# First conditioning in five steps of 2, 4, 4, 4 and 2 k-tiles, with the small loads on another queue and another transpose of x

## The chip, the cores and the metric

The kernel runs on one core of a Trainium2 chip. Its engines are TensorE (PE in the views; PEld is its weight load), VectorE (DVE), ScalarE (ACT), GpSimd (POOL) and SyncE (SP, which here only issues transfers). The metric is the device time of one launch in microseconds (us), the median of several runs.

## The reference, cut to what matters

One decoder block on 256 rows (SEQ) of width 2048 (D_MODEL), everything in float32. The change touches only the beginning: the conditioning vector c gives shifts, scales and gates through one large matrix, and the first of two SwiGLU networks reads the normalised and modulated x.

```python
def rms_norm(x, g):
    xf = x.astype(jnp.float32)
    y = xf * lax.rsqrt(jnp.mean(xf * xf, -1, keepdims=True) + EPS)
    return (y * g.astype(jnp.float32)).astype(x.dtype)
def modulate(x, g, shift, scale):
    return rms_norm(x, g) * (1 + scale) + shift
def swiglu(x, w_gate, w_up, w_down):
    return (jax.nn.silu(x @ w_gate) * (x @ w_up)) @ w_down
...
cond = jax.nn.silu(c)
ada = (cond @ w_ada[l] + b_ada[l]).reshape(B, N_ADA, 1, D)
sh1, sc1, gt1, sh2, sc2, gt2, sh3, sc3, gt3 = [ada[:, i] for i in range(N_ADA)]
h = modulate(x, g_norm[l, 0], sh1, sc1)
x = x + 0.5 * gt1 * swiglu(h, w_ffn_gate[l, 0], w_ffn_up[l, 0], w_ffn_down[l, 0])
```

The contraction of both w_ffn_gate and w_ffn_up runs over the 2048 columns of h, that is over 16 k-tiles of 128. A k-tile of h needs its own 128 shifts and 128 scales, which need all 2048 rows of 256 columns of w_ada.

## The kernel before

**Units.** Weights come in pieces of two k-tiles by 512 columns (512 KB), each into one of six `raw` buffers (`RAW`). ScalarE rounds a piece to its high part `whi` (L135), VectorE forms the low part `wlo` (L136), and TensorE multiplies: for each of two row halves of x and each of two k-tiles, the products whi·ahi, wlo·ahi and whi·alo (L215 to L217 from the function `unit`, L620 to L622 in `early`). That is 12 matmuls of 128x512, called a unit below. Four pairs of `whi` and `wlo` exist (`PREP`).

**Conditioning.** A piece of w_ada is not multiplied on TensorE: VectorE multiplies it by one column of cond and adds it to an accumulator `aacc` (L342 for the first of 16 row tiles, L344 for the other 15). At the end TensorE sums `aacc` over the partitions by matmuls with a column of ones (L379), VectorE adds the bias and the gain (L372, L373, result `mod`), and the function `mk` makes ahi (ScalarE, L717), the same in full (L719) and alo (VectorE, L724) from the transposed x. Such a chain of 16 pieces, a reduction and a `mk` is one step of the conditioning.

**Steps.** `STEPS` cuts the 16 k-tiles of the first network into four steps of four. Before the first step nothing can be multiplied. While the matmuls of one step run (nine half-chunks of weights, `EARLY`, so 18 units for four k-tiles), the 16 w_ada pieces of the next step are dealt out between the units by `interleave`, whose last two arguments (`LEAD`) say how many pieces are given at the outset. The first two half-chunks stay in PSUM over all steps, the other seven are emptied after each step (L625 on ScalarE after the first step, L627 on VectorE, which adds them up, after later ones).

**Order.** The program order is written out by hand: every engine works through its instructions in the order in which `run` emits them. `run` prepares pieces up to four ahead of the unit that is emitted (`AHEAD`), and a "bar" item holds preparation back at one place. A transfer into a `raw` buffer is issued by SP when the piece six before it has been used up.

**The beginning.** SP issues the loads of the identity, c, x and the w_ada pieces, and between these the eight small loads (biases, gains and positions, `load_small`, L299). ScalarE squares x (L434); the reduction, GpSimd's power and two diagonal matrices `dg` follow (`rstd_first`, L692 on VectorE), and `turn` multiplies x by `dg` on TensorE, which scales and transposes in one (L705). `small_cols` transposes the small loads (L304) and copies them (L305, L306).

Of the kernel before, what the change touches and what calls it, by code (L numbers as in the profile page):

```python
# [18 lines left out]
P = 128  # L19
D = 2048  # L20
# [15 lines left out]

LEAD = (0,3)
BAR, BARS = (2,0)
FILL = (4, 40, 320, 50, 60, 10)
XN = (0,14,0)  # L40
MK = 1
POOLN = 0
# [5 lines left out]
GAPS = (2, 4, 3, 2)  # L48
STEPS = ((0,4),(4,4),(8,4),(12,4))
C_ID, C_D, C_BC, C_MC, C_END = 0, 128, 384, 384 + 2 * HEADS * NCMP, 384 + 2 * HEADS * NCMP + 2 * NCMP  # L50
# [22 lines left out]
def block_kernel(ctx: ExitStack, tc: tile.TileContext, I, konst, decay, out):  # L73
# [10 lines left out]
    def act_hi(dt=F32R):  # L84
        return ap_.tile([P, 4, S], dt, tag="ahi", name="ahi")
# [30 lines left out]

    items, micro, held = [], deque(), []

# [15 lines left out]
    def split(raw_ap, hi_ap, lo_ap):  # L134
        nc.scalar.activation(hi_ap, raw_ap, AF.Copy)  # L135
        nc.vector.tensor_tensor(lo_ap, raw_ap, hi_ap.bitcast(F32), op=ALU.subtract)  # L136

    def run():
# [26 lines left out]
        def prep():  # L165
            i = st["prep"]
            kind, _, nk, n, fn = stream[i]
            raw = raws.pop(i)
            if kind == "w":
                hi = wp.tile([P, 2 * NCH], F32R, tag="whi", name="whi")  # L170
                lo = wp.tile([P, 2 * NCH], F32R, tag="wlo", name="wlo")
                split(raw[:, :nk * n], hi[:, :nk * n], lo[:, :nk * n])
                parts[i] = shaped(hi, nk, n), shaped(lo, nk, n)
                st["w"] += 1
            else:
                fn(raw[:, :nk * n])
            freed.add(i)
            st["prep"] += 1
            dma()
# [101 lines left out]
    nc.tensor.transpose(ps0[:, 0:16], r0[0:16], ident[0:16, 0:16])  # L281
    nc.scalar.activation(cond, ps0[:, 0:16], AF.Silu)

    def load_more():
# [13 lines left out]
                   (r2[102:118], I["ret_gn_gain"][0].rearrange("h (a p) -> (h a) p", p=P))]  # L298
    load_small = [("do", lambda to=to, frm=frm: nc.sync.dma_start(to, frm)) for to, frm in load_small]  # L299

# [19 lines left out]
    def rsqrt_mean(o, ssq, n):  # L320
# [3 lines left out]
        nc.gpsimd.tensor_tensor(o, o, mhalf[:, :w], op=ALU.pow)  # L324

    for t in range(2):
        nc.sync.dma_start(x[:, t], x_d[t * P:(t + 1) * P, :])
# [235 lines left out]
    def ffn(l, his, los, last, first=None, head=None):  # L563
# [84 lines left out]
        if first:  # L648
            its += first(*STEPS[0])
            for i, (k0, nk) in enumerate(STEPS):  # L650
                w = [it for ci in range(EARLY) for it in early(ci, k0, nk)]
                if i + 1 < len(STEPS):
                    w = interleave(w, first(*STEPS[i + 1]), int(len(w) * SPREAD), *LEAD)
                its += w
# [27 lines left out]

    big = cp.tile([P, 2, D], F32, tag="big", name="dg")
    dg = big[:, 0, :S].rearrange("p (t s) -> p t s", t=2)

    def rstd_first():
        for t in range(2):
            for n in range(4):
                square(t, n)
        r = rstd_x()  # L690
        for t in range(2):
            nc.vector.tensor_scalar(dg[:, t], ident, r[:, t:t + 1], None, op0=ALU.mult)  # L692

    h1, l1 = [], []

    def first(k0, nk):
        banks = []

        def turn():

            for k in range(nk):
                if k % 2 == 0:
                    banks.append(mx([P, 2, S]))
                for t in range(2):
                    nc.tensor.matmul(banks[-1][:, k % 2, t * P:(t + 1) * P], x[:, t, (k0 + k) * P:(k0 + k + 1) * P],  # L705
                                     dg[:, t], start=True, stop=True)

        def mk():
            h32 = t4([P, 4, S])
            for k in range(nk):  # L710
                kt = k0 + k
                if kt % 4 == 0:
                    h1.append(act_hi())
                    l1.append(act_lo())
                a, b = mod[:, 1, kt:kt + 1], mod[:, 0, kt:kt + 1]
                xT = banks[k // 2][:, k % 2]
                nc.scalar.activation(h1[-1][:, kt % 4], xT, AF.Identity, scale=a, bias=b)  # L717
                if MK:
                    nc.scalar.activation(h32[:, k], xT, AF.Identity, scale=a, bias=b)  # L719
                else:  # L720
                    nc.vector.tensor_scalar(h32[:, k], xT, a, b, op0=ALU.mult, op1=ALU.add)
                if k % 2:
                    ks = slice(kt % 4 - 1, kt % 4 + 1)
                    nc.vector.tensor_tensor(l1[-1][:, ks], h32[:, k - 1:k + 1], h1[-1][:, ks].bitcast(F32), op=ALU.subtract)  # L724
        o = ada_cols(0, k0, nk, True)
        if k0 == 0:
            o.insert(XN[1], ("do", small_cols))
            o.insert(XN[0], ("do", rstd_first))
            o = [i for it in zip(load_small, o) for i in it] + o[len(load_small):]
        if k0 == STEPS[1][0]:  # L730
            o.insert(5, ("do", load_more))
        o.insert(len(o) - 1 - XN[2], ("do", turn))
        return o + [("do", mk)] + ([("bar", BAR)] if k0 < BARS else [])

# [514 lines left out]
```

## Time and profile before

| | us |
|---|---|
| median of three runs | 2503.04 (2503.02 to 2503.77) |
| profiled execution, its own time | 2505.49 |
| its span, first to last instruction | 2503.7 |
| TensorE busy in the span | 2445.5 (98%) |
| VectorE busy | 1737.4 (69%) |
| ScalarE busy | 1140.9 (46%) |
| mean granted TensorE clock | 0.996 |

How to read it: the span is shorter than the execution by 1.8 us at its ends. TensorE is busy nearly throughout, so what shortens the kernel is its idle time, and its matmuls at the lower clock. A timeline row gives the start, the time from start to end of the merged instructions, the engine, the line, the operation and how many were merged; in brackets stand the idle time of the engine ahead of it and what ended that. Matmuls overlap in the rows: the time of one in a stream is the difference of the starts, 0.216 us at the higher level of the clock.

### The profile page before, as it was taken

To read this page: it belongs to the slowest core of one execution; us is meant where nothing else is said; L and a number is where in the kernel's file an instruction comes from. 1 tells how busy PE (TensorE), PEld (TensorE's weight loads), DVE (VectorE), ACT (ScalarE), POOL (GpSimd) and SP (SyncE) were. 2 spreads that over 40 slices of the span, in tenths; PEclk is the share of its full clock that TensorE was granted. 3 is DMA by queue.
4 is the path that set the end of the run, shared out by engine and by line. 5 is a ranking of instruction groups with operands and counts; after the bars stand their busy time and mean duration, and the time that the engine had idled before them with its cause. 6 is when DMAs were issued, how large, how long until landed. Compare 5 with 4: busy or idle time off the path is not lost. (4 is left out here: it accounts for less than half of the span.)

```text
span 2503.7 us, 31546 instructions
## 1 busy us (share of the span) xinstructions
PE 2445.5 (98%) x11616; PEld 2120.0 (85%) x11616; DVE 1737.4 (69%) x1968; ACT 1140.9 (46%) x1416; POOL 233.5 (9%) x201
## 2 busy tenths in 40 slices
PE   4999999999999999999999999999999999999999
PEld 4888888888887888888888888888788888888888
DVE  7898777898756466776767777776688555555555
ACT  3545444444445355554444444444544444444443
POOL 0000000110002133320000000001100010001001
PEclk9999999999999999999999999999999999999999
DMA  9998888899866455667888877887499666666664
GB/s 347 350 321 277 280 301 293 305 311 344 280 222 196 140 158 143 185 195 261 280 264 262 256 246 235 294 273 250 153 320 352 198 203 199 200 199 203 200 202 153
DMA packets 348339, 616.64 MB, mean 246 GB/s; under 512 B 22044, under 2 KB 80018, under 8 KB 347928
## 3 DMA queue, kind: packets, MB, share of 16 engines
q1 hardware_dynamic: 348184, 614.63, 74.8%
q8 instruction: 91, 1.49, 0.2%
q14 instruction: 64, 0.52, 0.1%
HBM read 612.45 MB, written 2.10 MB: 245 GB/s over the span
## 5 line engine op out<-in xcount | busy, mean ns | idle before, releaser
L136 DVE TENSOR_TENSOR wlo<-raw,whi 128x1024 fp32r<-128x1024 f32 (+1 forms) x865 | 1082.1, 1260 | 575.4 <-ACT whi L135 570.4
L135 ACT ACTIVATE whi<-raw 128x1024 fp32r<-128x1024 f32 (+1 forms) x865 | 906.9, 1056 | 1002.2 <-PE accb L217 730.6
L215 PE MATMUL accb<-whi,ahi 128*128 128x512 f32 x3232 | 1240.5, 384 | 6.1 <-ACT ahi L494 4.7
L216 PE MATMUL accb<-wlo,ahi 128*128 128x512 f32 x3232 | 1229.4, 380 | 3.8 <-DVE wlo L136 3.5
L217 PE MATMUL accb<-whi,alo 128*128 128x512 f32 x3232 | 1228.4, 380 | 2.9 <-DVE alo L541 1.5
L215 PEld LDWEIGHTS accb<-whi,ahi 128*128 128x128 f32 x3232 | 612.8, 190 | 95.1 <-ACT ahi L494 5.5
L216 PEld LDWEIGHTS accb<-wlo,ahi 128*128 128x128 f32 x3232 | 613.0, 190 | 92.2 <-DVE wlo L136 8.0
L217 PEld LDWEIGHTS accb<-whi,alo 128*128 128x128 f32 x3232 | 612.7, 190 | 92.5 <-DVE alo L541 1.9
L344 DVE SCALAR_TENSOR_TENSOR aacc<-raw,cond,aacc 128x1024 f32<-128x1024 f32 x270 | 354.2, 1312 | 1.3 <-DMA raw<-in_w_ada_dram 0.6
L558 POOL TENSOR_TENSOR x<-x,t 128x512 f32<-128x512 f32 x50 | 80.9, 1639 | 1156.2 <-DVE t L556 989.0
L621 PE MATMUL accb<-wlo,ahi 128*128 128x512 f32 x224 | 87.1, 389 | 2.5 <-DVE wlo L136 2.5
L620 PE MATMUL accb<-whi,ahi 128*128 128x512 f32 x224 | 86.7, 387 | 0.0
L622 PE MATMUL accb<-whi,alo 128*128 128x512 f32 x224 | 85.9, 384 | 0.0
L621 PEld LDWEIGHTS accb<-wlo,ahi 128*128 128x128 f32 x224 | 43.0, 192 | 12.1 <-DVE wlo L136 6.2
L540 ACT ACTIVATE ahi<-mx 128x512 fp32r<-128x512 f32 x52 | 28.1, 593 | 53.9 <-PE mx L449 53.9
L541 DVE TENSOR_TENSOR alo<-mx,ahi 128x512 fp32r<-128x512 f32 x52 | 33.4, 684 | 27.2 <-ACT ahi L540 27.2
L620 PEld LDWEIGHTS accb<-whi,ahi 128*128 128x128 f32 x224 | 43.1, 192 | 6.1
L622 PEld LDWEIGHTS accb<-whi,alo 128*128 128x128 f32 x224 | 43.0, 192 | 6.0
L556 DVE TENSOR_TENSOR t<-accb,gt 128x512 f32<-128x512 f32 x56 | 36.3, 683 | 7.7 <-PE accb L217 7.6
L787 ACT ACTIVATE t<-accb 128x512 f32<-128x512 f32 x52 | 30.1, 593 | 24.2 <-PE accb L217 24.1
L1004 ACT ACTIVATE t<-t,m 128x256 f32<-128x256 f32 (+1 forms) x64 | 28.3, 443 | 26.0 <-DVE m L994 26.0
L1113 POOL TENSOR_SCALAR rs<-bmv 128x2 f32<-128x2 f32 x8 | 1.8, 220 | 395.3 <-DVE bmv L1112 395.2
(182 smaller groups left out, 1025.6 us busy)
## 6 DMA issues: line engine op xcount, KB each, us to landing
raw<-in_w_ada_dram SPq DMA_DIRECT2D x288, 512.0 KB, 5.5
raw<-in_w_ffn_gate_dram SPq DMA_DIRECT2D x176, 512.0 KB, 5.1
raw<-in_w_ffn_up_dram SPq DMA_DIRECT2D x176, 512.0 KB, 4.7
raw<-in_w_ffn_down_dram SPq DMA_DIRECT2D x176, 512.0 KB, 4.2
raw<-in_w_in_dram SPq DMA_DIRECT2D x176, 512.0 KB, 4.5
raw<-in_w_in_dram SPq DMA_DIRECT2D x128, 256.0 KB, 3.9
raw<-in_w_proj_nsa_dram SPq DMA_DIRECT2D x32, 512.0 KB, 5.7
raw<-in_w_proj_ret_dram SPq DMA_DIRECT2D x32, 512.0 KB, 5.4
```

The costliest lines, as they stand in the source:

```text
L135: nc.scalar.activation(hi_ap, raw_ap, AF.Copy)
L136: nc.vector.tensor_tensor(lo_ap, raw_ap, hi_ap.bitcast(F32), op=ALU.subtract)
L215: nc.tensor.matmul(ps[t], xh, wh, start=kt == 0, stop=False)
L216: nc.tensor.matmul(ps[t], xh, wl, start=False, stop=False)
L217: nc.tensor.matmul(ps[t], xl, wh, start=False, stop=kt == K - 1)
L344: nc.vector.scalar_tensor_tensor(box[0], raw, k, box[0], op0=ALU.mult, op1=ALU.add)
L541: nc.vector.tensor_tensor(lo[:, 2 * b:2 * b + 2], ps, h.bitcast(F32), op=ALU.subtract)
L556: nc.vector.tensor_tensor(in_two(y), halves(ps[t]), in_two(gt[:, n * NCH:(n + 1) * NCH]), op=ALU.mult)
L558: (nc.vector if last and n == 3 else nc.gpsimd).tensor_tensor(xs, xs, y, op=ALU.add)
L620: nc.tensor.matmul(ps, xh, h, start=i == 0, stop=False)
L621: nc.tensor.matmul(ps, xh, l, start=False, stop=False)
L622: nc.tensor.matmul(ps, xl, h, start=False, stop=i == nk - 1)
```

## The change

Five things are changed together, all at the beginning of the program.

- `STEPS` becomes (0,2), (2,4), (6,4), (10,4), (14,2): five steps. In the first and last step the w_ada pieces are 2 x 256 columns (256 KB, runs of 1 KB instead of 2 KB) and each half-chunk has one unit. `LEAD` is given for each step; the second step's pieces get no head start.
- The eight small loads are issued by ScalarE's queue, ahead of the Silu that makes cond. `small_cols` and the squares become the first items of the program.
- x is scaled by ScalarE (`xs`, with the column rx) and transposed plainly against the identity, in place of the product with a diagonal matrix. The reduction of the squares stands behind six w_ada pieces on VectorE.
- Twelve matmuls of ones by ones, whose result nobody reads, stand behind the first transposes (`WARM`).
- In the first step `mk` forms alo for one k-tile at a time, and the first weight piece's wlo is emitted inside it; the bar now holds one piece behind the first step only.

```diff
-LEAD = (0,3)
-BAR, BARS = (2,0)
+LEAD = ((0, 0), (0, 3), (0, 3), (0, 3))
+BAR = 1
+WARM = 12
-XN = (0,14,0)
-MK = 1
+XN = (2, 5)
-STEPS = ((0,4),(4,4),(8,4),(12,4))
+STEPS = ((0, 2), (2, 4), (6, 4), (10, 4), (14, 2))
...
-                split(raw[:, :nk * n], hi[:, :nk * n], lo[:, :nk * n])
+                if st["w"]:
+                    split(raw[:, :nk * n], hi[:, :nk * n], lo[:, :nk * n])
+                else:
+                    nc.scalar.activation(hi[:, :nk * n], raw[:, :nk * n], AF.Copy)
+                    first_lo.append(lambda: nc.vector.tensor_tensor(
+                        lo[:, :nk * n], raw[:, :nk * n], hi[:, :nk * n].bitcast(F32), op=ALU.subtract))
...
-    load_small = [("do", lambda to=to, frm=frm: nc.sync.dma_start(to, frm)) for to, frm in load_small]
+    for to, frm in load_small:
+        nc.scalar.dma_start(to, frm)
...
+    nc.scalar.activation(cond, ps0[:, 0:16], AF.Silu)
...
+    def rms_first():
+        nc.vector.tensor_reduce(rx, ss, axis=AX.X, op=ALU.add)
+        rsqrt_mean(rx, rx, D)
...
+            ks = slice(k0 * P, (k0 + nk) * P)
+            for t in range(2):
+                nc.scalar.activation(xs[:, t, ks], x[:, t, ks], AF.Copy, scale=rx[:, t:t + 1])
             for k in range(nk):
                 if k % 2 == 0:
                     banks.append(mx([P, 2, S]))
                 for t in range(2):
-                    nc.tensor.matmul(banks[-1][:, k % 2, t * P:(t + 1) * P], x[:, t, (k0 + k) * P:(k0 + k + 1) * P],
-                                     dg[:, t], start=True, stop=True)
+                    nc.tensor.transpose(banks[-1][:, k % 2, t * P:(t + 1) * P],
+                                        xs[:, t, (k0 + k) * P:(k0 + k + 1) * P], ident)
+            if k0 == 0:
+                ps = mx()
+                for _ in range(WARM):
+                    nc.tensor.matmul(ps, ones_r, ones_r[:, None, :].to_broadcast([P, 4, P]), start=True, stop=True)
...
+            n = 1 if k0 == 0 else 2
...
+                while first_lo:
+                    first_lo.pop()()
...
+        if k0 == 0:
+            o.insert(XN[1], ("do", turn))
+            o.insert(XN[0], ("do", rms_first))
+            o = [("do", small_cols), ("do", lambda: [square(t, n) for t in range(2) for n in range(4)])] + o
+            return o + [("do", mk), ("bar", BAR)]
+        o.insert(len(o) - 1, ("do", turn))
+        return o + [("do", mk)]
```

Where the instructions stand: first VectorE from the program's beginning to the first low part of weights (`rx` is the column of 1/rms, `dg` the diagonal matrices, `cols` the small loads). Before:

```order
L438 TENSOR_REDUCE rx<-ss 128x2
L692 TENSOR_SCALAR dg<-kc,rx 128x128 x2
L342 TENSOR_SCALAR aacc<-raw,cond 128x1024
L344 SCALAR_TENSOR_TENSOR aacc<-raw,cond,aacc 128x1024 x15
L136 TENSOR_TENSOR wlo<-raw,whi 128x1024
```

The multiplications of the w_ada pieces stood behind the norm of x. And after, the same place on VectorE:

```order
L310 COPY cols<-mx 128x128 x2
L311 TENSOR_SCALAR gq<-cols 128x1
L348 TENSOR_SCALAR aacc<-raw,cond 128x512
L350 SCALAR_TENSOR_TENSOR aacc<-raw,cond,aacc 128x512 x5
L693 TENSOR_REDUCE rx<-ss 128x2
L350 SCALAR_TENSOR_TENSOR aacc<-raw,cond,aacc 128x512 x10
L378 TENSOR_TENSOR mod<-mx,cols 128x2x2
L379 SCALAR_TENSOR_TENSOR mod<-mod,cols 128x2
L176 TENSOR_TENSOR wlo<-raw,whi 128x1024
```

They now stand behind the small loads, each has half the columns, and the norm has moved behind the sixth. Second, SP's queue from the load of x on. Before, once the first step's pieces and the small loads are issued:

```order
L162 DMA raw<-in_w_ffn_gate_dram 128x2x512
L162 DMA raw<-in_w_ada_dram 128x2x512 x4
L162 DMA raw<-in_w_ffn_gate_dram 128x2x512
L162 DMA raw<-in_w_ada_dram 128x2x512
L162 DMA raw<-in_w_ffn_up_dram 128x2x512
```

One w_ada piece of the next step came with each unit's weights. After:

```order
L333 DMA x<-in_x_dram 128x2048 x2
L162 DMA raw<-in_w_ada_dram 128x2x256 x16
L162 DMA raw<-in_w_ffn_gate_dram 128x2x512
L162 DMA raw<-in_w_ada_dram 128x2x512 x2
L162 DMA raw<-in_w_ffn_up_dram 128x2x512
L162 DMA raw<-in_w_ada_dram 128x2x512 x2
```

In the first step now two w_ada pieces come with each unit's weights: 16 pieces of the next step with nine units instead of with 18.

## Rows read from the trace of the kernel before

**Rows 1.** The page, busy time of the engines over the span.

```profile
PE 2445.5 (98%) x11616; PEld 2120.0 (85%) x11616; DVE 1737.4 (69%) x1968; ACT 1140.9 (46%) x1416; POOL 233.5 (9%) x201
```

**Rows 2.** Timeline, the beginning: start, length, engine, line, operation, count.

```profile
6.52 0.63 ACT L434 ACTIVATE t<-x 128x512 f32<-128x512 f32 x1 [2.71 <-DMA x<-in_x_dram]
...
12.85 0.48 DVE L692 TENSOR_SCALAR dg<-kc,rx 128x128 f32<-128x128 f32 x2 [1.11 <-POOL rx L324]
...
14.03 19.77 DVE L344 SCALAR_TENSOR_TENSOR aacc<-raw,cond,aacc 128x1024 f32<-128x1024 f32 x15
...
35.50 3.41 PE L379 MATMUL mx<-ones,aacc 128*128 128x1 f32 x16
...
39.41 0.56 ACT L717 ACTIVATE ahi<-mx,mod 128x256 fp32r<-128x256 f32 x1 [5.58 <-DVE mod L373]
...
40.03 0.80 PE L215 MATMUL accb<-whi,ahi 128*128 128x512 f32 x1 [1.12 <-ACT ahi L717]
...
43.13 0.63 PE L216 MATMUL accb<-wlo,ahi 128*128 128x512 f32 x1
```

**Rows 3.** Timeline of TensorE, later: clock reached, step 2's reduction, steps' first matmuls, end.

```profile
47.66 0.38 PE L215 MATMUL accb<-whi,ahi 128*128 128x512 f32 x1
...
88.80 1.84 PE L379 MATMUL mx<-ones,aacc 128*128 128x1 f32 x16
...
95.76 0.38 PE L215 MATMUL accb<-whi,ahi 128*128 128x512 f32 x1
...
152.13 0.38 PE L215 MATMUL accb<-whi,ahi 128*128 128x512 f32 x1
...
203.83 0.38 PE L215 MATMUL accb<-whi,ahi 128*128 128x512 f32 x1
...
254.88 0.38 PE L622 MATMUL accb<-whi,alo 128*128 128x512 f32 x1
```

**Rows 4.** Windows: stretch, length, busy of PE, PEld, DVE, ACT, POOL; clock; DMA share; GB/s.

```profile
20.00:24.00 4.00, 0.00 (x0) 0.00 (x0) 3.89 (x4) 0.00 (x0) 0.00 (x0) 1.00 1.05 384
48.00:92.00 44.00, 43.38 (x216) 37.73 (x215) 35.57 (x32) 22.72 (x29) 0.00 (x0) 1.00 1.02 371
...
1257.00:1262.00 5.00, 5.00 (x25) 4.38 (x24) 4.13 (x6) 2.11 (x2) 0.00 (x0) 1.00 0.82 236
1309.00:1315.00 6.00, 6.00 (x29) 5.26 (x28) 4.18 (x4) 2.29 (x3) 0.00 (x0) 1.00 0.97 325
```

**Rows 5.** Line L299, the small loads: issue time on SP (ns min/median/max); landing.

```profile
L299 SPq DMA_DIRECT2D t<-in_b_ada_dram x3: 333/457/1114, 7.3 to 19.7; - x3
...
DMA to landing us min/median/max: 10.0/10.0/10.0
```

**Rows 6.** VectorE's groups by form: count, busy, mean ns, idle before.

```profile
L344 DVE SCALAR_TENSOR_TENSOR aacc<-raw,cond,aacc 128x1024 f32<-128x1024 f32 x270 | 354.2, 1312 | 1.3 <-DMA raw<-in_w_ada_dram 0.6
...
L627 DVE TENSOR_TENSOR t<-accb,t 128x512 f32<-128x512 f32 x18 | 11.6, 679 | 1.4 <-PE accb L622 1.4
...
L886 DVE SCALAR_TENSOR_TENSOR t<-t 128x128 f32<-128x128 f32 x48 | 14.1, 298 | 1.9 <-ACT t L787 0.4
```

**Rows 7.** Timeline of TensorE around two later gaps, and eight plain transposes.

```profile
245.27 0.48 PE L621 MATMUL accb<-wlo,ahi 128*128 128x512 f32 x1 [1.21 <-DVE wlo L136]
245.59 0.38 PE L622 MATMUL accb<-whi,alo 128*128 128x512 f32 x1
...
487.33 1.04 PE L449 MATMUL mx<-kc,t 128*128 128x128 f32 x8
...
490.78 0.48 PE L217 MATMUL accb<-whi,alo 128*128 128x512 f32 x1 [1.47 <-DVE alo L541]
...
491.84 0.63 PE L217 MATMUL accb<-whi,alo 128*128 128x512 f32 x1
```

**Rows 8.** Windows, the step from 96 to 151 (columns as in rows 4).

```profile
96.00:151.00 55.00, 53.24 (x243) 45.33 (x242) 49.96 (x52) 24.09 (x28) 0.00 (x0) 0.94 0.92 325
```

**Rows 9.** Timeline of VectorE, a wait inside `mk`.

```profile
93.09 0.69 DVE L724 TENSOR_TENSOR alo<-t,ahi 128x512 fp32r<-128x512 f32 x1 [2.06 <-ACT t L719]
```

More of the change, by code (lines that the diff above doesn't have):

```diff
@@ L114, in in_two @@
         return ap.rearrange("p (h j) -> p h j", h=2)
-    items, micro, held = [], deque(), []
+    items, micro, held, first_lo = [], deque(), [], []
     def weights(src, nk, n, fn):
@@ L281, in block_kernel @@
     nc.tensor.transpose(ps0[:, 0:16], r0[0:16], ident[0:16, 0:16])
-    nc.scalar.activation(cond, ps0[:, 0:16], AF.Silu)
     def load_more():
@@ L652, in ffn @@
                 if i + 1 < len(STEPS):
-                    w = interleave(w, first(*STEPS[i + 1]), int(len(w) * SPREAD), *LEAD)
+                    w = interleave(w, first(*STEPS[i + 1]), int(len(w) * SPREAD), *LEAD[i])
                 its += w
@@ L680, in ffn @@
         return its
[L683 to L692, printed above, removed]
+    xs = cp.tile([P, 2, D], F32, tag="big", name="xs")
+    rx = cp.tile([P, 2], F32, name="rx")
+    def rms_first():
+        nc.vector.tensor_reduce(rx, ss, axis=AX.X, op=ALU.add)
+        rsqrt_mean(rx, rx, D)
     h1, l1 = [], []
@@ L704, in turn @@
                 for t in range(2):
-                    nc.tensor.matmul(banks[-1][:, k % 2, t * P:(t + 1) * P], x[:, t, (k0 + k) * P:(k0 + k + 1) * P],
-                                     dg[:, t], start=True, stop=True)
-        def mk():
[L709 to L724, printed above, removed]
+                    nc.tensor.transpose(banks[-1][:, k % 2, t * P:(t + 1) * P],
+                                        xs[:, t, (k0 + k) * P:(k0 + k + 1) * P], ident)
@@ new lines, in turn @@
+            if k0 == 0:
+                ps = mx()
+                for _ in range(WARM):
+                    nc.tensor.matmul(ps, ones_r, ones_r[:, None, :].to_broadcast([P, 4, P]), start=True, stop=True)
+        def mk():
+            n = 1 if k0 == 0 else 2
+            for k in range(0, nk, n):
+                h32 = t2([P, 2, S])
+                for i in range(n):
+                    kt = k0 + k + i
+                    if kt % 4 == 0:
+                        h1.append(act_hi())
+                        l1.append(act_lo())
+                    a, b = mod[:, 1, kt:kt + 1], mod[:, 0, kt:kt + 1]
+                    xT = banks[(k + i) // 2][:, (k + i) % 2]
+                    nc.scalar.activation(h1[-1][:, kt % 4], xT, AF.Identity, scale=a, bias=b)
+                    nc.scalar.activation(h32[:, i], xT, AF.Identity, scale=a, bias=b)
+                while first_lo:
+                    first_lo.pop()()
+                ks = slice((k0 + k) % 4, (k0 + k) % 4 + n)
+                nc.vector.tensor_tensor(l1[-1][:, ks], h32[:, :n], h1[-1][:, ks].bitcast(F32), op=ALU.subtract)
@@ L725, in first @@
         o = ada_cols(0, k0, nk, True)
+        if k0 == STEPS[2][0]:
+            o.insert(5, ("do", load_more))
         if k0 == 0:
[L727 to L733, printed above, removed]
+            o.insert(XN[1], ("do", turn))
+            o.insert(XN[0], ("do", rms_first))
+            o = [("do", small_cols), ("do", lambda: [square(t, n) for t in range(2) for n in range(4)])] + o
+            return o + [("do", mk), ("bar", BAR)]
```

## The prediction

> **What bounds the kernel now.** I read the page's busy times first: TensorE is busy for 2445.5 of 2503.7 us [rows 1], so 58 us are idle, and all that the change can give lies in them or in matmuls at the lower clock. The timeline of the beginning shows where most of them are: the first weight matmul starts at 40.03 [rows 2]. What ends last there: the squares of x, the reduction and GpSimd's power let VectorE go on at 12.85, and then VectorE multiplies w_ada pieces without a pause until 14.03 + 19.77 = 33.8. So the start is bound by VectorE: 16 pieces at some 1.3 us each, begun late because the norm of x stands ahead of them. Behind it come TensorE's reduction (35.50, 3.41 us long, held up by the transposes that stand in front of it), the addition of the bias, and the first ahi at 39.41.
>
> From there to 255.1 (the last early matmul starts at 254.88) the four steps run. Their first matmuls stand at 40.03, 95.76, 152.13 and 203.83 [rows 2, 3], so they took 55.7, 56.4, 51.7 and 51.3 us. One unit is 12 x 0.216 = 2.59 us, 18 of them 46.6 us; the rest of a step is the turn, the reduction (1.84 us), short waits for wlo and stretches at the lower clock. The other engines are close behind: in the step from 96 to 151 VectorE is busy for 49.96 of 55 us [rows 8], and from 48 to 92 the transfers run at 371 GB/s with a DMA share of 1.02 [rows 4], which is about what they reach at all (384 GB/s from 20 to 24). This is what decides the case: behind the start there are three bounds within a few us of each other.
>
> **The change part by part.**
>
> *The start.* The first half of x is in at 6.5 [rows 2], so transfers begin near 3 us, and x (2.1 MB at 384 GB/s) is through by 8.6; the small loads, 0.1 MB, add 0.3. Then come 16 pieces of 256 KB, 4.19 MB. At 384 GB/s they take 10.9 us. But their runs are 1 KB; the stretches nearest to that moved 236 GB/s at a share of 0.82 and 325 at 0.97 [rows 4], that is 288 and 335 per full share, or some 300 here: 14.0 us. VectorE's time for a piece of 512 columns lies between 0.298 us (128 columns) and 1.312 us (1024) [rows 6]; on the line through both it is 0.73, some 0.65 back to back, so VectorE is no longer the bound, the transfers are. With half a us to land and one multiplication behind the last, the sums are through at T = 8.9 + 10.9 + 1.15 = 21.0 or 24.0; I take 22.8, nearer the slower rows. VectorE may begin only when the small loads are in, transposed and copied. Eight issues at about 0.45 us [rows 5] from 2.4 on end at 6, and they land at 9 to 11, about when the first piece lands (9.9). The Silu for cond now waits behind these issues, until 7.3, and the eight squares at 0.63 us end at about 12.3, in time for the reduction behind the sixth piece (14). That move costs nothing while T is set by transfers; without this cover it would cost the 3.7 us by which cond is later.
>
> The Trainium skill, in DMA: Bandwidth & Descriptors, Rules for kernel authors, wants transfers of at least 1 MiB for full bandwidth, and its Bandwidth table gives 0.95 us for 64 KB and 6.15 us for 1 MB. An estimate on the line between them is 2.0 us for each of these pieces, 32 us in all, by which T would be 42 and the time 2513. By the same line the 512 KB pieces of the kernel before would need 3.4 us each; the trace moves one in 1.37 us, with six in flight.
>
> *The turn and the twelve idle matmuls.* rx is ready at about 15.5, xs at 16.5, the four transposes end by 18, and twelve matmuls at 0.43 us (the difference of the starts at the lower clock) end by 23.2. That is T, near enough; at T = 21 they would hold the reduction up by 2 us. Behind T: eight matmul entries of the reduction, half of 1.84 us, or half of 3.41 at the lower clock; 0.4 us for the bias, 0.6 for the first ahi. The first weight matmul stands at F = T + 3 = 26, between 24 and 28. That is 14 us earlier than 40.03. I count nothing more for the clock: 0.63 instead of 0.38 us lasted from 40.03 to 47.4, and cost 15 x 0.21 = 3.2 us, but in the new first step TensorE waits for transfers anyway.
>
> *The new first step.* It has nine units, 23.3 us, but 16 pieces of the next step come with them, and these must be in before the second step. Behind the first step's own pieces 24 transfers of 512 KB (eight of weights, 16 of w_ada) come before the last w_ada piece: 12.6 MB at 375 GB/s are 33.5 us. The first step's pieces are through at T - 0.8 = 22, so the last w_ada piece lands at 56, is multiplied by 57.4, reduced by 59.3, and ahi stands at 60.3. TensorE runs the ninth unit meanwhile and starts the second step at 62. VectorE alone would need as long: 25 wlo and w_ada pieces at 1.2 to 1.3 us [rows 6] are 30 to 32 us from T + 4 on. So TensorE, 14 us earlier at the start, waits some 10 us in this step.
>
> *The second step* (18 units, 16 pieces of w_ada) starts without a lead: the transfer of its second weight piece is sixth behind the last w_ada piece and lands at 66.5, and its wlo is ready at 69, when TensorE would want it at 64.6. That and a second wait like it cost 4 to 5 us; then 46.6 + 2.8 for turn and reduction + 0.5: 54.5, at 116.5. *The third* (the same counts, buffers filled ahead): as the third step before, 51.7, with 1 us less for the turn, since eight transposes of one pass take 1.04 [rows 7] and the products have two passes; and 1 us more for short waits: 51.5, at 168. *The fourth* carries only half-size pieces, which VectorE does in 16 x 0.65 instead of 16 x 1.3 us: 46.6 + 1.9 + 1 = 49.5, at 217.5. *The fifth*: 23.3, and the 4.7 us that the last step before took over its units: 28, at 245.5. VectorE has one more round of sums to add (14 x 0.68 = 9.5 us [rows 6]), which the fourth step's 10 us less of multiplying make room for.
>
> 245.5 instead of 255.1 is 9.6 us. Behind it the program is the same on TensorE, which is busy for nearly all of it, so the gain stays. Against the profiled execution: 2505.5 - 9.6 = 2495.9; the runs' median lies 2.45 us lower, so 2493.4, say **2493**.
>
> **The rivals.**
>
> *Fed better.* Transfers at 384 GB/s with no cost for 1 KB runs: T = 21, the second step at 59.5, no wait for its second piece, steps of 50.5, 50.5, 49 and 28: end at 237.5, gain 17.6, **2485**. For it: 384 and 371 GB/s in full stretches. Against it: nothing in these steps leaves a lead.
>
> *The steps stay bound by VectorE or by transfers.* The second and third step take what the second took before, 56.4, and what VectorE needs, 53.5 (49.96 busy [rows 8] and some 3.5 of waiting in `mk`, 2.06 of it in one piece [rows 9]); the fourth 51.7, the fifth 29. From 62 the end is at 252.6: gain 2.5, **2500.5**. For it: VectorE's 91%. Against it: a clock of 0.94 over those 55 us [rows 8] says that 3 us of the 56.4 were the lower level.
>
> *A late start.* Small loads that land as slowly as on SP's queue (10.0 us from issue to landing [rows 5]) are in at 16, VectorE begins at 18 and ends at 30, T is 7 us later; the rest follows, less 2 us that the second step then waits less: gain 4.6, **2498.4**. Against it: those rows stood in a queue behind six large pieces, these do not.
>
> *Half-size pieces no quicker than whole ones* (16 x 1.37 = 21.9 us): T = 32, gain 0.5, **2502.5**. This decides for slower from 1.41 us a piece on, and each further 0.1 us costs 1.6. The 1 KB stretches of rows 4 speak against it: 0.8 to 0.9 us a piece.
>
> *The lower clock through the first step.* A unit takes 5.1 us at 0.427 us a matmul. If the waits between units, 1.5 us each, put TensorE at the lower level for all nine units, the turn and the reduction (26 + 46 + 5.5), the second step starts at 77.5 and, with the transfers then ahead, ends 3.5 us shorter: end at 257.4, **2505.4**, slower than before by 2.4; with the second step's beginning at the lower level too, 2508.6. It decides from all nine units on: one such unit costs 1 us more than the 4.1 us in which its pieces arrive. For it: behind a gap of 1.47 us the matmuls fell to 0.63 us. Against it: behind 1.21 us they stayed at 0.38 [rows 7], and a unit at the lower level has no gap behind it, after which the level came back within 7.4 us in every such row.
>
> The Trainium skill, in TensorE: Matmul & The Clock Gate, section HAM oscillation — how this bites in real kernels, speaks for that rival: matmul bursts shorter than the waits for the next slice of data restart at the lower clock each time. Its bursts (2 us against waits of 3 to 5) are the reverse of these (2.6 against 1.5), and the trace's gap of 1.21 us kept the higher level; by the rule the time is 2505 to 2509.
>
> **How the numbers follow.** Forecast (gain of 5 to 15, 2488 to 2498) 0.62; fed better 0.09; steps bound as before 0.14; late start 0.06; half-size pieces slow 0.04; lower clock 0.05. About 0.2%, 5 us, is what a measurement can tell from no change. Faster by more: 0.62 + 0.09 + 0.04 of the third + 0.04 of the late start = 0.79; slower: 0.02 of the slow pieces and 0.02 of the clock = 0.04; the same 0.17. The range 2486 to 2501 leaves out half of the fed-better case, the clock, most of the slow pieces and the edge of the third, under 0.2.
>
> **What would show it.** In the new trace: the w_ada multiplications end at 21 to 24, the first weight matmul stands at 24 to 28, the nine units of the first step lie 3.5 to 4.5 us apart with waits for wlo or whi, the second step starts at 59 to 65, and the last early matmul stands near 245. The twelve idle matmuls end before or at T. It would be wrong if the first w_ada multiplication stands behind 14, if the granted clock is 0.5 over most of 26 to 60, or if the second step starts after 70.

## The result

The changed kernel takes 2523.2 us (median of four runs, 2521.2 to 2527.7) against 2503.15 for the kernel before: ratio 1.0083, 95% interval [1.0069, 1.0096]. It is slower by 20 us; forecast were 2493, in a range from 2486 to 2501, with a chance of 0.04 for slower.

The page of the kernel after, its span and its busy line ([rows 1] before):

```profile
span 2525.9 us, 31618 instructions
PE 2460.8 (97%) x11596; PEld 2125.9 (84%) x11596; DVE 1744.1 (69%) x1999; ACT 1147.0 (45%) x1426; POOL 237.5 (9%) x201
```

TensorE is busy for 15 us more, 4.5 of them in the twelve idle matmuls, and idle for 7 us more. The profiled execution took 2527.7 us, the slowest of the four (2505.5 for the kernel before), so what a place costs below is read from one execution, and all places together make 22 us instead of 20.

The beginning in the timeline of after (columns as in [rows 2]; L220 is what L215 was, L626 what L620 was, L385 the reduction):

```profile
12.16 0.49 DVE L348 TENSOR_SCALAR aacc<-raw,cond 128x512 f32<-128x512 f32 x1
18.76 0.91 ACT L705 ACTIVATE xs<-x,rx 128x256 f32<-128x256 f32 x2 [4.68 <-POOL rx L329]
20.27 4.54 PE L715 MATMUL mx<-ones_r 128*128 128x512 f32 x12
20.93 3.99 DVE L350 SCALAR_TENSOR_TENSOR aacc<-raw,cond,aacc 128x512 f32<-128x512 f32 x5 [0.18 <-DMA raw<-in_w_ada_dram]
24.98 1.05 PE L385 MATMUL mx<-ones,aacc 128*128 128x1 f32 x8 [0.16 <-DVE aacc L350]
27.33 0.79 PE L220 MATMUL accb<-whi,ahi 128*128 128x512 f32 x1 [1.30 <-ACT ahi L728]
```

So the start is what the change wanted: the first weight matmul stands at 27.33 instead of 40.03 [rows 2]. The gain is gone by the end of the early matmuls. To see where, I numbered the units from 0 (12 weight matmuls each, the same amount of work in both kernels) on TensorE's timeline and took the difference of their starts, after minus before:

| unit | 1 | 7 | 9 | 24 | 27 | 42 | 45 | 60 | 63 | 68 | 72 | 75 | 96 |
|---|---|---|---|---|---|---|---|---|---|---|---|---|---|
| us | -13.6 | -5.8 | +6.2 | +4.4 | +12.2 | +4.2 | +10.5 | +5.2 | +13.4 | +12.8 | +17.9 | +23.8 | +23.4 |

The first unit, number 0, stands at -12.7. Units 1 to 7 lose 7.8 us to the supply, as forecast. Then there are four jumps, at units 7 to 9, 24 to 27, 42 to 45 and 60 to 63, where a step turns into the next, and one more over units 68 to 75, in the last step and just behind it. (It falls in between wherever the kernel before has a turn of its own.) From unit 82 on the difference hardly moves: the program is the same there.

What TensorE waited for from 20 to 300 (engine, line, releaser: us in total, times, longest):

```profile
PE mx L710 <- ACT xs L705: 8.6, 7, 3.6
PE accb L627 <- DVE wlo L136: 6.2, 10, 0.8
PE accb L626 <- ACT whi L135: 5.2, 4, 3.7
PE accb L220 <- ACT whi L135: 2.5, 1, 2.5
```

In the kernel before, TensorE's longest wait from 40 to 300 was 1.2 us. The first line is new: the transposes of a turn wait for xs. The first turn in the timeline:

```profile
57.90 2.60 DVE L350 SCALAR_TENSOR_TENSOR aacc<-raw,cond,aacc 128x1024 f32<-128x1024 f32 x2
60.29 1.06 ACT L135 ACTIVATE whi<-raw 128x1024 fp32r<-128x1024 f32 x1 [2.59 <-DMA raw<-in_w_ffn_gate_dram]
61.58 1.06 ACT L135 ACTIVATE whi<-raw 128x1024 fp32r<-128x1024 f32 x1 [0.23 <-DMA raw<-in_w_ffn_gate_dram]
62.54 1.07 ACT L631 ACTIVATE t<-accb 128x512 f32<-128x512 f32 x2
63.50 1.33 ACT L705 ACTIVATE xs<-x,rx 128x512 f32<-128x512 f32 x2
64.27 0.33 PE L710 MATMUL mx<-kc,xs 128*128 128x128 f32 x1 [3.59 <-ACT xs L705]
66.43 3.41 PE L385 MATMUL mx<-ones,aacc 128*128 128x1 f32 x16
69.70 0.77 PE L626 MATMUL accb<-whi,ahi 128*128 128x512 f32 x1
74.89 0.38 PE L220 MATMUL accb<-whi,ahi 128*128 128x512 f32 x1
```

The sums are complete at 60.50 and TensorE's last product ends at 60.7. But xs, which needs nothing but x and rx and could have been made from 18.8 on, stands in ScalarE's queue behind two conversions that wait for their transfers and an evacuation. TensorE pauses for 3.59 us and falls to the lower level: the reduction takes 3.41 instead of 1.84 us [rows 3] and the ninth unit 5.2 instead of 2.6. The windows of after show it (PE, PEld, DVE, ACT, POOL busy, granted clock, DMA share, GB/s; 0.50 is 1.2 GHz):

```profile
60.00:64.00 4.00, 0.68 (x4) 0.25 (x2) 3.06 (x4) 3.48 (x5) 0.00 (x0) 1.00 1.04 389
64.00:68.00 4.00, 3.45 (x17) 3.27 (x17) 1.84 (x2) 0.83 (x2) 0.00 (x0) 0.57 1.04 380
68.00:72.00 4.00, 4.00 (x15) 3.55 (x16) 0.33 (x2) 1.66 (x4) 0.00 (x0) 0.50 0.70 260
72.00:76.00 4.00, 4.00 (x14) 3.29 (x13) 2.57 (x3) 3.48 (x8) 0.00 (x0) 0.65 0.00 0
```

The last row shows a second price of the late turn: the transfers stand still as well (0 GB/s), since ScalarE converts the next pieces only behind `mk`.

The turn into the fifth step looks alike: here the sums are there at 224.3, and xs stands behind a conversion whose transfer lands at 229.7.

```profile
223.60 0.74 DVE L350 SCALAR_TENSOR_TENSOR aacc<-raw,cond,aacc 128x512 f32<-128x512 f32 x1
229.66 1.06 ACT L135 ACTIVATE whi<-raw 128x1024 fp32r<-128x1024 f32 x1 [1.54 <-DMA raw<-in_w_ffn_up_dram]
230.62 0.90 ACT L705 ACTIVATE xs<-x,rx 128x256 f32<-128x256 f32 x2
231.17 1.10 PE L710 MATMUL mx<-kc,xs 128*128 128x128 f32 x4 [3.04 <-ACT xs L705]
```

Behind it lies the last loss. In the narrow last step a half-chunk ends with every unit, so a Silu of a gate sum (L647) comes every second unit. It waits for VectorE's additions, the next conversions stand behind it, and TensorE waits for these:

```profile
262.14 1.06 ACT L647 ACTIVATE ahi<-ahi 128x1024 f32<-128x1024 f32 x1 [6.50 <-DVE ahi L633]
263.10 1.99 ACT L135 ACTIVATE whi<-raw 128x1024 fp32r<-128x1024 f32 x2
264.19 0.48 PE L626 MATMUL accb<-whi,ahi 128*128 128x512 f32 x1 [3.66 <-ACT whi L135]
281.20 0.48 PE L220 MATMUL accb<-whi,ahi 128*128 128x512 f32 x1 [2.49 <-ACT whi L135]
```

### The profile page after: what moved, and what is told of

Read it like the earlier page. It is cut to its first block, busy times and chain, and to the rows that moved or that the text cites. A ratio compares the mean times of both kernels' runs of the same rounds, so it can differ in the third digit from the quotient of the medians.

```text
span 2525.9 us, 31618 instructions
## 1 busy us (share of the span) xinstructions
PE 2460.8 (97%) x11596; PEld 2125.9 (84%) x11596; DVE 1744.1 (69%) x1999; ACT 1147.0 (45%) x1426; POOL 237.5 (9%) x201
## 5 line engine op out<-in xcount | busy, mean ns | idle before, releaser
L136 DVE TENSOR_TENSOR wlo<-raw,whi 128x1024 fp32r<-128x1024 f32 x864 | 1076.5, 1256 | 581.0 <-ACT whi L135 572.9
L135 ACT ACTIVATE whi<-raw 128x1024 fp32r<-128x1024 f32 x864 | 906.3, 1056 | 1004.9 <-PE accb L222 733.6
L220 PE MATMUL accb<-whi,ahi 128*128 128x512 f32 x3232 | 1241.0, 384 | 8.9 <-ACT ahi L500 4.5
L220 PEld LDWEIGHTS accb<-whi,ahi 128*128 128x128 f32 x3232 | 612.9, 190 | 99.1 <-ACT ahi L500 5.3
L350 DVE SCALAR_TENSOR_TENSOR aacc<-raw,cond,aacc 128x1024 f32<-128x1024 f32 (+1 forms) x285 | 356.4, 1251 | 1.7 <-DMA raw<-in_w_ada_dram 0.8
L626 PE MATMUL accb<-whi,ahi 128*128 128x512 f32 x224 | 90.6, 404 | 5.3 <-ACT whi L135 5.2
L626 PEld LDWEIGHTS accb<-whi,ahi 128*128 128x128 f32 x224 | 44.9, 200 | 14.4 <-ACT whi L135 7.7
L547 DVE TENSOR_TENSOR alo<-mx,ahi 128x512 fp32r<-128x512 f32 x52 | 33.4, 684 | 29.2 <-ACT ahi L546 29.2
```

What stands on the lines that cost most here:

```text
L220: nc.tensor.matmul(ps[t], xh, wh, start=kt == 0, stop=False)
L350: nc.vector.scalar_tensor_tensor(box[0], raw, k, box[0], op0=ALU.mult, op1=ALU.add)
L547: nc.vector.tensor_tensor(lo[:, 2 * b:2 * b + 2], ps, h.bitcast(F32), op=ALU.subtract)
L626: nc.tensor.matmul(ps, xh, h, start=i == 0, stop=False)
```

## The experiments

Theory Q was that the in-order queue of ScalarE makes the losses, rival N that the narrow steps starve TensorE anyway. Ratios are to the kernel before, run on the same chip; the changed kernel has 1.0083. A sentence such as "the turn costs 6 us" speaks of the differences of unit starts as above, from one trace each.

**xs one step ahead.**

```diff
+    def scaled(i):
+        k0, nk = STEPS[i]
...
-            for t in range(2):
-                nc.scalar.activation(xs[:, t, ks], x[:, t, ks], AF.Copy, scale=rx[:, t:t + 1])
+            if k0 == 0:
+                scaled(0)
...
+            i = STEPS.index((k0, nk)) + 1
+            if i < len(STEPS):
+                scaled(i)
```

`scaled` takes over the lines that the turn loses, for step i; the last lines stand at the end of `mk`.

> The changed kernel, but ScalarE scales the x of a step one step earlier, right behind the products of the step before. Theory Q (the turn waits in ScalarE's queue: xs stands behind conversions of weights that wait for transfers): the waits of the turn for xs (8.6 us, 7 times) go, the reduction starts as soon as the sums are there (60.5 at the first turn, 224.3 at the last), TensorE keeps its higher level, and the four turns cost some 16 us less: 2507 (2502 to 2512). Rival N (the narrow steps starve TensorE anyway, and xs is only what it happens to wait for last): the wait moves to the reduction, 2520 to 2524.

2517.0 us, ratio 1.0054 [1.0039, 1.0069]: 7 us back, fewer than Q's 16. The time lies between Q's range and N's. The waits of TensorE from 20 to 310:

```profile
PE accb L627 <- DVE wlo L136: 5.8, 9, 0.8
PE accb L626 <- ACT whi L135: 5.0, 5, 3.7
PE accb L220 <- ACT whi L135: 3.6, 2, 2.5
PE mx L385 <- DVE t L633: 3.4, 2, 1.7
```

The waits for xs are gone. The first turn (units 7 to 9) costs 5.9 instead of 12.0 us against before (3.9 us of that are lost again by unit 11, since the pieces of the second step are not yet in), the last (60 to 63) 1.2 instead of 8.2. The second and third turn cost what they did (7.8 and 6.2), and the fourth line says why: the wait has moved. The second turn of this kernel, and behind it the second turn of the kernel before:

```profile
114.34 3.49 DVE L136 TENSOR_TENSOR wlo<-raw,whi 128x1024 fp32r<-128x1024 f32 x3
115.86 1.04 PE L715 MATMUL mx<-kc,xs 128*128 128x128 f32 x8
117.74 1.29 DVE L633 TENSOR_TENSOR t<-accb,t 128x512 f32<-128x512 f32 x2
118.58 2.73 PE L385 MATMUL mx<-ones,aacc 128*128 128x1 f32 x16 [1.68 <-DVE t L633]
121.17 0.77 PE L626 MATMUL accb<-whi,ahi 128*128 128x512 f32 x1
```

```profile
139.02 1.95 PE L705 MATMUL mx<-dg,x 128*128 128x128 f32 x16
141.74 2.35 PE L379 MATMUL mx<-ones,aacc 128*128 128x1 f32 x16 [0.77 <-DVE t L627]
```

The reduction needs a PSUM bank that VectorE's additions (L633) set free, and these stand behind three wlo. The plain transposes are through in 1.04 us instead of the products' 1.95 and only wait longer, 1.68 instead of 0.77 us before. The granted clock is then 0.50 from 120 to 124.

**The Silu a unit later.**

```diff
                 elif up:
                     g = sg.pop(c)
+                    nc.scalar.activation(g, g, AF.Silu)
                     nc.gpsimd.tensor_tensor(z, z, g, op=ALU.mult)
                     push(*[None] * GAPS[1], transposed(c, z))
                 else:
-                    nc.scalar.activation(z, z, AF.Silu)
+                    if ci + 1 == EARLY:
+                        nc.scalar.activation(z, z, AF.Silu)
                     sg[c] = z
```

> The changed kernel, but the Silu of an early gate sum is issued with the finish of the up sum, one unit later. In the last step (two k-tiles) such a Silu stands in ScalarE's queue in front of the next conversions once in two units, and waits there for VectorE's additions. Theory Q: 8 of the 10.5 us that units 65 to 76 lose go: 2514 to 2517. Rival N: VectorE is the bound of that step (per unit 1.2 for wlo, 1.3 for two additions, 0.6 for the alo of the transposed sums, 0.6 for w_ada: 3.7 of 2.6 us), so nothing changes: 2521 to 2525.

2520.3 us, ratio 1.0071 [1.0056, 1.0086], between Q's range and N's. In the trace the fifth step takes 25.6 us instead of 31.6, and 4.4 us are then lost on before within the next six units (5.5 in the changed kernel): 7 us back at this place, near Q's 8. But the medians differ by 3 us only, and the two intervals overlap. What the place of the Silu costs by itself is not settled by this run; that it is not all of the loss is.

**Four steps again**, `STEPS = ((0, 4), (4, 4), (8, 4), (12, 4))` in the changed kernel.

> The changed kernel with the steps of the kernel before (four of 4 k-tiles). The first sums are 16 pieces of some 1.3 us from 12.2 on, so the first weight matmul stands near 36.5 instead of 40.0. Theory Q: the three turns wait for xs as they do in the changed kernel and cost some 2 to 3 us more each than before: 2503 to 2508. Rival N (the loss is in the steps of two k-tiles): the gain of the start stays, 2498 to 2501.

2517.3 us, ratio 1.0058 [1.0041, 1.0074]. Worse than either expected. TensorE gains 4.9 us at the start (unit 3), and waits for xs in every turn: 2.1 us in the first, 0.7 in the second, 5.6 in the third. The first turn costs 6.6 us more than before's and the third 9.5; the second, with its short wait, costs 1.7 less. So the change of the turn loses without any narrow step, and N as the only cause falls.

**The steps alone**, the five steps in the kernel before.

> The kernel before with the steps of 2, 4, 4, 4, 2 k-tiles and nothing else: turns by products with the diagonal, small loads by SP's queue, the norm of x ahead of the sums. The first sums take 16 x 0.73 instead of 16 x 1.3 us, first weight matmul near 31. Theory Q: the turns wait for nothing on ScalarE, the gain of 9 is partly eaten by the first step's supply (some 6) and by the last step's Silu (some 8): 2504 to 2510. Rival N: as the changed kernel or worse, 2520 to 2530.

2519.2 us, ratio 1.0068 [1.0053, 1.0083]. That is just below N's range and far from Q's. So the narrow steps lose without xs as well; there are at least two causes. The start gains 4.2 us only (first weight matmul at 35.78): the sums are through at 26.5, but the copies of the small loads, which the bias needs, stand on VectorE at 31.6, behind a wlo and a w_ada piece, and `mod` is there at 35.1.

**The diagonal turn** in the changed kernel, dg made by ScalarE behind rx.

> The changed kernel, but the turn is the product with a diagonal again (the kernel before's way; ScalarE scales the unit matrix once, behind rx), so no turn waits for ScalarE. Theory Q (the waits for xs in ScalarE's queue): as with xs one step ahead, the first turn costs 6 us less and the last 5 us less; and since two-pass products take 1.95 instead of 1.04 us, TensorE waits less for the reduction's bank (VectorE's additions, 1.7 us with xs ahead): 2510 to 2515. Rival C (the pauses of each turn, whatever they wait for, put TensorE at the lower level): turns cost as in the changed kernel, 2519 to 2524.

2516.7 us, ratio 1.0054 [1.0037, 1.0071]: as xs ahead. The first turn costs 5.9, the second 6.2, the third 4.9 and the last 1.7 us against before. The time lies between Q's range and C's, but the first and the last turn are as Q had them: Q holds for xs, by a second way of taking it out.

**The reduction in front of the transposes**, with xs ahead.

```diff
-        o.insert(len(o) - 1, ("do", turn))
-        return o + [("do", mk)]
+        return o + [("do", turn), ("do", mk)]
```

> xs one step ahead, and in each later turn the reduction of the sums stands in front of the transposes instead of behind them. With xs ahead the second and third turn still cost 7.9 and 6.2 us: the reduction waits 1.7 us for a bank that VectorE's additions leave, these stand behind three wlo, and the level falls behind that wait. Theory V (that wait is what is left of the turns' cost): the reduction takes a bank that is free, mod and ahi come some 2 us earlier, the transposes cover the wait, the second and third turn cost 4 to 5 us less each: 2506 to 2511. Rival C (the low activity of a turn lowers the level in any order): 2515 to 2519 as with xs ahead alone.

2514.2 us, ratio 1.0045 [1.003, 1.006], between V's range and C's. The same place as above:

```profile
114.95 1.84 PE L385 MATMUL mx<-ones,aacc 128*128 128x1 f32 x16
116.65 0.63 PE L715 MATMUL mx<-kc,xs 128*128 128x128 f32 x4
117.67 1.06 PE L715 MATMUL mx<-kc,xs 128*128 128x128 f32 x4 [0.38 <-DVE t L633]
118.38 0.78 PE L626 MATMUL accb<-whi,ahi 128*128 128x512 f32 x1
```

The wait is 0.38 instead of 1.68 us, the next unit starts 3.4 us after the turn's first instruction instead of 5.3, and the second turn costs 4.7 instead of 7.8 us. The median is 2.8 us lower than with xs ahead alone; the two intervals overlap, so the size rests on the trace.

**Diagonal turn and four steps**: of the change only the new beginning is left.

> The changed kernel with four steps of 4 k-tiles and the turn by products with the diagonal: what is left of the change is the small loads by ScalarE's queue, the norm behind the sixth piece, the idle matmuls and the order of the lo halves. Theory Q: the 3.4 to 5 us of the earlier start stay, since the turns wait for nothing new: 2497 to 2501, against 2517 for four steps with scaled x. Rival C: three turns at the lower level as with four steps and scaled x: 2508 to 2517.

2504.1 us, ratio 1.0002 [0.9992, 1.0011]. No loss and no gain, between Q's range and C's. TensorE is 4.8 us ahead at unit 3, loses 2.3 in unit 4 (it waits 0.99 us for whi and 0.78 for wlo, that is for supply) and the rest in small pieces up to unit 54, 2.0 of it in the third turn; from there on it is behind by 0.7.

**The three together**: xs ahead, reduction in front, Silu later.

> xs one step ahead, the reduction in front of the transposes, and the Silu of a gate sum one unit later. If the three losses are separate (turns waiting for xs, turns waiting for a bank, conversions behind Silu in the last step), the profile's shift against the kernel before ends near 13.8 - 9 - 8 = -3: 2498 to 2504. If they overlap, or the narrow steps are bound by supply, 2508 to 2514.

2511.3 us, ratio 1.003 [1.0018, 1.0041]. The second of the two expectations came. At unit 69 TensorE is ahead of before (-1.4); by unit 75 it has lost 7.6 us (+6.2). From unit 68 to 82 it loses 7.2 us, against 9.7 without the later Silu. The second turn costs 3.3 us instead of 4.7 with the same instructions and the same wait of 0.38 us: here the granted clock stayed at 1.00, which the Silu has no part in. So the 4 us between the two ratios are not the Silu's alone, and their intervals overlap.

**The gate's w_ada pieces 12 units later**, on top of the three.

```diff
-    items.extend(interleave(f1[w0:w1_], fill, w1_ - w0 - FILL[0]))
+    items.extend(interleave(f1[w0:w1_], fill, w1_ - w0 - FILL[0], 12))
```

> The three together (xs ahead, reduction in front, Silu later), and the w_ada pieces of the gate, which began inside the last narrow step, begin 12 units later. With the three together units 69 to 76 still lose 7 us, and VectorE has no pause from 237 to 257 there. Theory E (in the last step VectorE is the bound: 1.2 us of wlo, 1.3 of additions, 0.6 of alo and 0.6 of w_ada per unit of 2.6 us): without the w_ada part 3 to 6 of the 7 us go, 2505 to 2509. Rival (the waits of that step are a chain between ScalarE and VectorE that w_ada has no part in, or the pieces only collide later): 2510 to 2514.

2502.2 us, ratio 0.9997 [0.9988, 1.0006]: 8 us by the ratios, more than E's 3 to 6, and in the trace the loss between units 69 and 75 is gone (-0.2 at both). The stretch from 237 to 257, of the three together and then of this kernel (columns as in the windows above):

```profile
237.00:257.00 20.00, 19.08 (x95) 16.27 (x94) 20.00 (x23) 8.67 (x10) 5.67 (x2) 1.00 0.74 234
```

```profile
237.00:257.00 20.00, 20.00 (x102) 17.66 (x101) 19.71 (x24) 10.29 (x11) 7.71 (x3) 1.00 0.65 202
```

VectorE was busy for all 20 us and is still busy for 19.7; with 0.7 us of w_ada in them instead of 4.5 the same 20 us carry 102 matmuls instead of 95, and TensorE has no pause. So VectorE was the bound of the last step. The w_ada pieces of the gate stood there in the kernel before too, and it was not run with this cure. But TensorE waits there for only 1.5 us in all from 203 to 256, so by an estimate from this wait the cure can give it about as much, not 8 us.

**No idle matmuls**, `WARM = 0` in the changed kernel.

> The changed kernel without the 12 idle matmuls. In the changed kernel they end at 24.8, the reduction starts at 24.98, and the granted clock is 0.50 from 28 to 32 in spite of them. If they hold nothing up and keep nothing up, 2521 to 2525 as the changed kernel; if they hold up the reduction, 1 us less; if the level fell earlier without them, the first units cost up to 3 us more.

2525.0 us, ratio 1.0079 [1.0063, 1.0095], as the changed kernel. In the time the twelve neither cost nor bring anything that can be measured. In the trace the reduction takes 1.87 us without them and 1.05 behind them, and the first weight matmul stands at 27.70 instead of 27.33. The two traces, at medians that are the same, also show how much of a place's cost belongs to one execution: the last turn costs 4.2 us here and 8.2 above, and 36 weight matmuls run at the lower level instead of 65.

**The three together with four steps.**

> The three together (xs ahead, reduction in front, Silu later) with four steps of 4 k-tiles. The diagonal with four steps gave 2504. Theory: three turns of some 4.8 us instead of 3.5, 7.9 and 4.0, the start 4 us earlier, no narrow step: 2498 to 2502, faster than both kernels. Rival (transposes that are done sooner only wait longer, as with xs ahead alone): 2503 to 2508.

2500.8 us, ratio 0.9986 [0.9976, 0.9996]: 2.9 us faster than the kernel before, as the theory had it, and the only run here whose interval lies below 1. TensorE is 2.1 us ahead at the start and 2.9 at unit 96: with the turns in order, the start's gain stays.

**Steps of 2, 2, 4, 4, 4**, with the three.

> The three together with steps of 2, 2, 4, 4, 4 k-tiles: the early start stays, the last step is wide again. Theory E: the 7 us of the narrow last step go, and the transfers of the first step fit (9 units, 16 half-size pieces: 8.9 MB, 23 us), but the second step then waits for its supply as the first did: 2502 to 2508. Rival (what a narrow step saves at the start it loses in any place): 2509 to 2514 as the three together.

2511.7 us, ratio 1.0029 [1.0018, 1.004], as the rival had it. The wide last step is no trouble any more (49.3 us for 18 units), the first step takes 34.2 us for its nine units, and the second 41.3: the narrow step that has to carry 16 full w_ada pieces starves in the second place as it did in the first (transfers at 354 GB/s and a DMA share of 1.00 from 63 to 104).

With all four cures the loss is gone. By the ratios they gave 7 us (xs), 2 (reduction), 4 (Silu) and 8 (w_ada), each on top of those before it; that these add up to the loss follows from their order and shows nothing by itself. The first (just) and the last are clear of noise in time, and both are clear in the trace. The 2 and the 4 are within the intervals, and part of the 4 is the clock.

## Why the prediction was wrong

First matmul of each step, from TensorE's timeline, and the end of the early matmuls:

| | step 1 | 2 | 3 | 4 | 5 | end |
|---|---|---|---|---|---|---|
| forecast | 26 | 62 | 116.5 | 168 | 217.5 | 245.5 |
| after | 27.33 | 74.89 | 132.28 | 186.49 | 241.37 | 273.00 |
| three cures | 28.20 | 67.18 | 123.98 | 178.42 | 227.97 | 254.24 |
| four cures | 28.47 | 67.96 | 125.08 | 179.53 | 229.83 | 254.80 |

*The start* was right, with a wrong bound. 24 to 28 was forecast, 27.33 came; the sums ended at 24.92 instead of 22.8. VectorE, not the transfers, set this: 16 pieces took 12.8 us with pauses of 0.25 and 0.18 only, 0.78 to 0.80 for each in a row. The line through [rows 6] had given 0.65 to 0.73. That 27.33 still lies in the range is partly luck: the sums were 2.1 us late, outside the 21 to 24 that were forecast, and the first weight matmul came 2.4 us behind them instead of 3. The half-size pieces came at 262 to 330 GB/s from 12 to 24, and VectorE began at 12.16, so neither the rival of the slow pieces nor that of the late start happened.

*The first step's nine units* were right: some 4 us apart, short of supply, the granted clock 1.00 from 36 to 60. The rival of the lower clock did not happen there. The second step's sums came at 60.50 instead of 57.4, 2 of these 3 us from the start.

*The turn* is the step that failed first: the second step started at 74.89 instead of 62, behind the 70 that I had named as a sign of being wrong. I wrote that the third step needs "1 us less for the turn", counting TensorE's instructions alone. The scaling that the change puts ahead of them was priced at the start, where ScalarE is idle, and not in the four later turns. There it is behind conversions that wait for transfers: 8.6 us of waiting in the trace, and as much again by the lower level. Start distances of 0.40 to 0.46 us show 65 weight matmuls at the lower level from 20 to 335, against 24 before and 13 with all four cures, each 0.21 us longer. Taking the scaling out of the turns gave 7 of these back, by two different ways; part of the rest moved to the wait for a bank. I had looked at what stands behind each new wait only for the Silu of cond, not for xs.

*That TensorE "runs the ninth unit meanwhile"* held. The forecast's 62 is the reduction's end, 59.3, and one unit of 2.6 us. In the trace the unit stands behind the reduction too (69.70 above), `mk` is done under it, and the second step follows at 74.89 without a gap. What failed is what stands ahead of it: nothing covers the transposes and the reduction, so each wait there is TensorE's own, and the unit ran at the lower level for 5.2 us.

*That a shorter turn saves time* was wrong in mechanism as well. With xs ahead the quicker transposes became a longer wait for the bank. The row was there to be read: before's own turns already waited for this, 0.77 us at 141.7 in one of them.

*The fifth step* was the second mis-sized term. I gave it 28 us and VectorE's extra sums 9.5 us, which I put into the fourth step's slack. But in a step of nine units all nine half-chunks end, so the additions, the alo of the transposed sums and the Silus come at twice the rate, and the gate's w_ada pieces on top. It took 31.6 us, and over five more were lost right behind it. With three cures it takes 26.3 and eight are lost behind it; with the w_ada pieces later it takes 25.0, and nothing to speak of is lost behind it.

*What is left.* With the four cures the early part ends at 254.8, not 245.5: 2.5 us at the start, 3.5, 2.6 and 2.9 in the first three steps and 0.8 in the fourth came on top, and the fifth gave 3 back. So even with the four cures the five steps gain nothing: of the 11.6 us of their earlier start 10.8 go into a first step that waits for transfers and carries one more turn. None of my rivals named ScalarE's queue. The one whose time was slower than before (2505.4) put the lower clock into the units of the first step, where it did not last; in the turns, where it came, it followed the waits. The range was too narrow because its ends came only from the supply and from VectorE's load. Whether the remaining 9 us could be won by another dealing of the pieces wasn't tried.

## What to carry to other kernels

An operation moved to another engine has to be priced at each place where it stands, by what that engine's queue waits for there, and not by its length. If it depends on early data, issue it early: scaling x one step ahead gave 7 us back at no cost. A narrow step is only cheap if the work that comes once a step (turn, sums, evacuations, Silus) and the pieces that the next step needs fit into its time on every engine; an earlier start is worth no more than the supply that follows.

## What the runs showed of the hardware

In a turn, pauses far below the 1.21 us of [rows 7] were followed by the lower level: 0.77 us in the kernel before (granted clock 0.50 from 144 to 148), and 0.38 us with the reduction in front (0.71 from 116 to 120), each between small matmuls (transposes, one-column products) and not in a stream of full ones. The Trainium skill, in TensorE: Matmul & The Clock Gate, section A second HAM failure mode: psum-queue depth-cycling, tells of short idle gaps between groups of matmuls, from cycling through PSUM banks, that make the clock go up and down. The 1.68 us for a bank with xs ahead, and 0.50 behind it, agree.

It does not happen each time. The second turn with the reduction in front, and then the same turn with the later Silu, which has the same instructions and the same 0.38 us:

```profile
116.00:120.00 4.00, 3.62 (x20) 3.14 (x20) 3.96 (x5) 0.00 (x0) 0.00 (x0) 0.71 0.99 344
```

```profile
116.00:120.00 4.00, 3.62 (x26) 3.10 (x26) 3.96 (x6) 0.00 (x0) 0.00 (x0) 1.00 0.92 296
```

The third turn with the diagonal waited 1.08 us and kept 1.00 as well (168 to 180). So the length of the pause alone does not tell whether the level falls; what else does is not shown here.

VectorE and GpSimd held each other up. Timeline of the three together:

```profile
242.30 1.28 DVE L547 TENSOR_TENSOR alo<-mx,ahi 128x512 fp32r<-128x512 f32 x2
242.53 2.38 POOL L645 TENSOR_TENSOR alo<-alo,ahi 128x1024 f32<-128x1024 f32 x1 [223.37 <-DVE alo L633]
243.50 2.49 DVE L350 SCALAR_TENSOR_TENSOR aacc<-raw,cond,aacc 128x1024 f32<-128x1024 f32 x1
```

The w_ada piece, 1.28 us elsewhere, takes 2.49 and ends 1.1 us behind GpSimd's product, as if it had begun when that ended. The two subtractions with an input in PSUM (L547), the second of which runs beside the product, keep their 1.28 us together. The Trainium skill, in SBUF — State Buffer, section SBUF: two separate sides, says that a VectorE operation with two inputs in SBUF and a GpSimd operation that reads SBUF exclude each other for a whole instruction; these rows agree. It makes VectorE's last step tighter still.
